# A fused matmul and batch norm on one core: an affine chain reordered, statistics taken in advance, and one output block moved behind the last matmul

## The chip, the cores and the metric

The kernel runs on one core of a Trainium2 chip. The metric is the device time of one execution in microseconds (us), told as the median of several. The profile shows one execution. Its span runs from the first to the last instruction and is about 1.8 us shorter than the time of the same execution (218.9 us against 220.69 before). A run is called slow when it lies over 1.5% above the fastest of its kernel.

Engines: PE is TensorE's matmuls, PEld its weight loads, DVE is VectorE, ACT is ScalarE, POOL is GpSimd, and SP issues the stores.

## The reference

```python
# x: 16 x 512 x 1024, weight: 1024 x 768, gamma, beta: 768, all float32
y = np.matmul(x, weight)
mean = np.mean(y, axis=(0, 1), keepdims=True)
var = np.var(y, axis=(0, 1), keepdims=True)
y_norm = (y - mean) / np.sqrt(var + eps)
return (gamma * y_norm + beta).astype(np.float32)     # 8192 rows x 768 columns, 25.2 MB
```

Each of the 768 columns needs its mean and variance over all 8192 rows before its first value can be stored.

## The kernel before

The columns are six tiles of 128 (nt = 0 to 5), the rows sixteen chunks of 512 (c). Tiles 0 to 2 are done first, with rows on the partitions. Their statistics end at about 126 us. From there on their output is made (VectorE multiplies by the scale, GpSimd adds the shift), while TensorE multiplies tiles 3, 4 and 5. Those three have their columns on the partitions, are normalized in place, transposed by TensorE, copied from PSUM to SBUF by ScalarE and stored. Every instruction is placed on its engine by an event with a time in a list that is sorted, so an event's time is an order and not a clock.

The affine numbers of a finished tile, and its normalization:

```python
def finish(nt):
    one = slice(nt, nt + 1)
    seq(nc.vector.bn_aggr(mv[:, nt, :], stats[:, nt, :, :]))
    seq(nc.scalar.activation(std[:, one], mv[:, nt, 1:2], AF.Sqrt, bias=eps_sb, scale=1.0))
    seq(nc.vector.scalar_tensor_tensor(
        tmp[:, one], mv[:, nt, 0:1], -1.0, gamma_sb[:, one], op0=ALU.mult, op1=ALU.mult,
    ))
    seq(nc.vector.reciprocal(rstd, std[:, one]))
    seq(nc.vector.tensor_mul(scale[:, one], rstd, gamma_sb[:, one]))
    seq(nc.vector.scalar_tensor_tensor(
        shift[:, one], tmp[:, one], rstd, beta_sb[:, one], op0=ALU.mult, op1=ALU.add,
    ))
# norm(nt, c, eng): y = y * scale + shift, in place, on VectorE ("dve") or ScalarE ("act")
# norm_rows: ring <- y * scale, VectorE.   shift_rows: ring <- ring + shift, GpSimd, in place.
```

The first affine chain, and the events of the three last tiles:

```python
S = pe
at(S + 0.9, affine_rows)                  # sums, scale, shift of tiles 0 to 2
at(S + 4.4, spread_rows, 0)               # scale as a row, by a matmul
for nt in range(GA):
    at(S + 2.4, norm, nt, 0, "dve")
at(S + 2.5, shift_diag)
at(S + 5.2, spread_rows, 1)               # shift as a row: GpSimd starts behind it
...
for b in range(C // 2):                   # outputs(nt, t0, step): tiles 3 and 4
    tb = t0 + step * b
    for i in range(2):
        at(tb - 2.2 + 0.5 * i, norm, nt, 2 * b + i, "act" if tb < tr + 2.0 and i == 0 else "dve")
    at(tb, turn_y, (nt,), 2 * b * CH, 2 * RT)
    at(tb + 2.2, out_copy, (nt,), 2 * b * CH, "act")
    at(tb + 2.3, store, (nt,), 2 * b * CH, 2 * RT)
```

```python
singles = ctx.enter_context(tc.tile_pool(name="singles", bufs=1))
xtpool = ctx.enter_context(tc.tile_pool(name="xtpool", bufs=C - EARLY))
...                                       # singles: 20 tiles in all; of these:
ones = singles.tile([P, P], f32)          # only column 0 is read
stats = singles.tile([P, NT, C, 6], f32)
msq = singles.tile([P, GA], f32)
...
if late:                                  # out_copy of tile 5
    o_sb = xtpool.tile([P, tiles, cols], f32, tag="xT")
else:                                     # all other outputs: pieces of the ring in singles
    o_sb = piece(tiles * cols).rearrange("p (s n) -> p s n", n=cols)
```

## Time and profile before

| | before |
|---|---|
| median of three runs (range) | 221.04 us (220.65 to 222.17) |
| span of the profiled run | 218.9 us |
| statistics of tiles 0 to 2 begin to be joined (S) | 126.48 us |
| last matmul ends (E) | 199.75 us |
| behind it, to the end of the span | 19.16 us |

S here and below is the measured start of the first aggregate of the first affine chain (the code's S is an event time), and the differences are taken from the trace's own times. The page's slices, 40 equal parts of 5.5 us, tenths busy for TensorE and GB/s of all transfers:

```profile
PE   7998999999999999999999979999999988995900
GB/s 60 175 204 190 194 196 196 197 196 196 194 191 197 195 196 196 198 189 10 0 4 0 0 0 14 340 308 257 269 258 360 295 353 334 346 346 347 201 345 244
```

The reader sees TensorE at 8 or 9 tenths nearly throughout, loads at about 196 GB/s in the first half, a pause of seven slices, and then stores that run at about 346 GB/s and break once (201), one slice behind the one where TensorE falls to 5.

### The profile page before, as it was taken

The numbers are of one execution on the slowest core, as the hardware profiler recorded it, in microseconds if no ns is written. First come the engines' busy times: TensorE is split into PE (matmuls) and PEld (weight loads), VectorE is DVE, ScalarE is ACT, GpSimd is POOL, SyncE is SP. The second block draws the span as 40 slices with busy tenths as digits, with TensorE's granted clock in tenths as the row PEclk, the third lists the DMA queues.
The fourth block names the chain that finished last, engine by engine and source line by source line (L and its number), as shares of the span: only waits on it lengthen the run. The fifth ranks groups of instructions, "written<-read, shape, count | busy, mean of one in ns | idle before, by whom it ended". The sixth has DMA issues, their size and how long they took to land.

```text
span 218.9 us, 3417 instructions
## 1 busy us (share of the span) xinstructions
PE 198.5 (91%) x1154; PEld 105.2 (48%) x1170; DVE 155.7 (71%) x264; ACT 119.8 (55%) x220; POOL 134.0 (61%) x153
## 2 busy tenths in 40 slices
PE   7998999999999999999999979999999988995900
PEld 3453545454544555546555534444444545651900
DVE  3223788897978789998554287889989999745800
ACT  2001454554543566636666225776676887985850
POOL 8897595977765799935559103999899953000000
PEclk9999999999999999999999999999999999999795
DMA  5999999999999999990000000986769899999698
GB/s 60 175 204 190 194 196 196 197 196 196 194 191 197 195 196 196 198 189 10 0 4 0 0 0 14 340 308 257 269 258 360 295 353 334 346 346 347 201 345 244
DMA packets 70161, 43.75 MB, mean 200 GB/s; under 512 B 4096, under 2 KB 69632, under 8 KB 70144
## 3 DMA queue, kind: packets, MB, share of 16 engines
q0 software_dynamic: 34624, 18.36, 61.1%
q1 hardware_dynamic: 35520, 25.18, 35.7%
q8 instruction: 9, 0.15, 0.3%
q14 instruction: 8, 0.07, 0.1%
HBM read 36.71 MB, written 25.17 MB: 283 GB/s over the span
## 4 chain that ended last, share of the span: by engine, by line
PE 64%; DVE 10%; POOL 8%; DMA 6%; issue 4%; ACT 3%; ACTq 0%; DVEq 0%; POOLq 0%
PE y_ps L190 31%; PE y_ps L180 29%; POOL ring L280 6%; PE o_ps L340 3%; ACT o_sb L353 3%; DVE stats L299 3%; DMA w_sb<-in_weight_dram 3%; DVE ring L274 2%; DVE y_sb L324 2%; DMA ring<-in_x_dram 2%; POOL w_sb L143 2%; DMA out_dram<-ring 1%; POOL ring L156 1%; DVE mv L306 1%; PE a_ps L266 1%
## 5 line engine op out<-in xcount | busy, mean ns | idle before, releaser
L190 PE MATMUL y_ps<-xT_sb,w_sb 128*128 128x512 bf16 (+1 forms) x477 | 117.5, 381 | 2.6 <-DMA w_sb<-in_weight_dram 1.4
L190 PEld LDWEIGHTS <-w_sb 128*128 128x128 bf16 x492 | 46.7, 96 | 60.8 <-issue 3.1
L302 ACT CAST y_sb<-y_ps 128x512 bf16<-128x512 f32 x60 | 35.4, 590 | 53.3 <-DVE stats L299 51.4
L180 PE MATMUL y_ps<-w_sb,xT_sb 128*128 128x384 bf16 x384 | 63.4, 326 | 0.0
L299 DVE BATCH_NORM_STATS2 stats<-y_ps 128x6 f32<-128x512 f32 x60 | 40.6, 684 | 22.5 <-PE y_ps L190 22.3
L280 POOL TENSOR_TENSOR ring<-ring,sum 128x768 f32<-128x768 f32 x24 | 43.5, 1847 | 17.9 <-ACT sum L268 14.0
L156 POOL DMA_DIRECT2D ring<-in_x_dram x72 | 45.2, 633 | 11.7 <-DVE xT_sb L168 6.1
L180 PEld LDWEIGHTS <-xT_sb 128*128 128x128 bf16 x384 | 37.5, 98 | 25.6
L206 POOL TENSOR_TENSOR sum<-sum,sq_sb 128x384 f32<-128x384 f32 x38 | 38.0, 1000 | 18.0 <-ACT sq_sb L202 16.8
L168 DVE STREAM_TRANSPOSE xT_sb<-ring 128x1024 f32<-128x1024 f32 (+1 forms) x34 | 39.5, 1167 | 12.0 <-DMA ring<-in_x_dram 12.0
L340 PE MATMUL o_ps<-ident,y_sb 128*128 128x128 bf16 x240 | 37.3, 230 | 5.5 <-DVE y_sb L324 5.2
L209 DVE TENSOR_TENSOR sum<-y_ps,sum 128x384 f32<-128x384 f32 x48 | 26.1, 544 | 14.6 <-ACT sq_sb L202 13.8
L202 ACT ACTIVATE sq_sb<-y_ps 128x384 f32<-128x384 f32 x48 | 23.4, 492 | 14.9 <-PE y_ps L180 11.4
L215 ACT CAST y_sb<-y_ps 128x384 bf16<-128x384 f32 x48 | 22.9, 476 | 7.5 <-DVE sum L209 7.3
L353 ACT CAST ring<-o_ps 128x1024 f32<-128x1024 bf16 (+1 forms) x24 | 22.5, 960 | 4.9 <-PE o_ps L340 2.5
L340 PEld LDWEIGHTS <-y_sb 128*128 128x128 bf16 x240 | 20.6, 104 | 9.1 <-DVE y_sb L324 7.3
L274 DVE TENSOR_TENSOR ring<-y_sb,a_ps 128x768 f32<-128x768 bf16 x24 | 22.3, 938 | 0.2 <-PE a_ps L266 0.2
L324 DVE TENSOR_SCALAR y_sb<-y_sb,scale,shift 128x512 bf16<-128x512 bf16 x43 | 17.3, 457 | 0.0
L319 ACT ACTIVATE y_sb<-y_sb,shift,scale 128x512 bf16<-128x512 bf16 x17 | 13.3, 813 | 0.1
L149 PE MATMUL idle_ps<-idle_sb 128*128 128x512 bf16 x37 | 9.8, 429 | 1.2 <-DVE idle_sb L100 1.2
L353 ACT CAST o_sb<-o_ps 128x512 f32<-128x512 bf16 x16 | 7.9, 679 | 1.2 <-PE o_ps L340 1.2
L149 PEld LDWEIGHTS <-idle_sb 128*128 128x128 bf16 x38 | 4.0, 108 | 6.4 <-issue 1.9
(45 smaller groups left out, 35.9 us busy)
## 6 DMA issues: line engine op xcount, KB each, us to landing
ring<-in_x_dram POOLq DMA_DIRECT2D x56, 256.0 KB, 8.5
out_dram<-ring SPq DMA_DIRECT2D x32, 384.0 KB, 2.9
out_dram<-ring SPq DMA_DIRECT2D x16, 512.0 KB, 5.9
out_dram<-o_sb SPq DMA_DIRECT2D x16, 256.0 KB, 3.3
ring<-in_x_dram POOLq DMA_DIRECT2D x16, 128.0 KB, 5.2
w_sb<-in_weight_dram POOLq DMA_DIRECT2D x8, 96.0 KB, 4.6
w_sb<-in_weight_dram POOLq DMA_DIRECT2D x4, 192.0 KB, 5.4
gamma_sb<-in_gamma_dram SPq DMA_DIRECT2D x6, 0.5 KB, 4.8
```

Of the source, the lines that this page charges most:

```text
L156: seq(nc.gpsimd.dma_start(x_bf[32 * i:32 * i + 32], src[:, :, KQ * i:KQ * (i + 1)]))
L168: seq(nc.vector.transpose(dst[:, half, :, jw0:jw1], src[:, :, jw0:jw1]))
L180: seq(nc.tensor.matmul(y_ps, xT[c][:, jw, s * P:(s + 1) * P, e], w_sb[:, jw, e, 0:NA], start=(jw == 0 and e == 0), stop=(jw == JW - 1 and ...
L190: seq(nc.tensor.matmul(y_ps, w_sb[:, jw, e, nt * P:(nt + 1) * P], xT[c][:, jw, q0 * QR:q1 * QR, e], start=(jw == 0 and e == 0 and q0 == 0) ...
L206: seq(eng.tensor_add(acc, acc, py.pop(("sq", c, s))))
L209: seq(nc.vector.tensor_add(sum1, py["row", c, s][:, 0:NA], sum1))
L274: seq(nc.vector.tensor_mul(o_sb, yrow[c][:, s:s + 2], aff[0][:, None, :].to_broadcast([P, 2, NA]),))
L280: seq(nc.gpsimd.tensor_add(o_sb, o_sb, sum1[:, None, :].to_broadcast([P, 2, NA])))
L299: seq(nc.vector.bn_stats(stats[:, nt, i, :], py[nt, c]))
L302: seq(nc.scalar.copy(y(nt, c), py.pop((nt, c))))
L340: seq(nc.tensor.transpose(dst, src, ident))
L353: seq(nc.scalar.copy(o_sb, src))
```

## The change

Its intent is to take waits off TensorE's path and to keep the stores going. Four parts: (1) in the first affine chain the three normalizations go behind the shift diagonals and the first rows' multiply, so that GpSimd starts earlier; (2) in the finishes of tiles 3 and 4, three one-element instructions go from VectorE to ScalarE; (3) the last 512 KB output block of tile 4 is held back and transposed behind the last matmul; (4) of tile 5, the statistics of fourteen chunks are joined ahead and the last chunk is multiplied and summed up by halves. Three small tiles are new. The core of the diff:

```diff
+    HELD = 1
...
     stats = singles.tile([P, NT, C, 6], f32)
+    ngamma = singles.tile([P, NT], f32)
+    nscale = singles.tile([P, 1], f32)
+    fin = singles.tile([P, 21], f32)
...
+    def sum_up():
+        seq(nc.vector.memset(fin[:, 0:1], float((C - 2) * CH)))
+        seq(nc.vector.bn_aggr(fin[:, 1:3], stats[:, NT - 1, 0:C - 2, :]))
+        seq(nc.vector.tensor_scalar(
+            fin[:, 2:3], fin[:, 2:3], float((C - 2) * CH), None, op0=ALU.mult))
...        (mm_half, bn_half, keep_half: the last chunk in two halves of 256)
+    def finish_var(nt):
+        one = slice(nt, nt + 1)
+        seq(nc.vector.bn_aggr(mv[:, nt, :], stats[:, nt, :, :]))
+        seq(nc.scalar.activation(std[:, one], mv[:, nt, 1:2], AF.Sqrt, bias=eps_sb, scale=1.0))
+        seq(nc.vector.reciprocal(rstd, std[:, one]))
+
+    def finish_affine(nt):
+        one = slice(nt, nt + 1)
+        seq(nc.scalar.activation(nscale, rstd, AF.Identity, scale=ngamma[:, one]))
+        seq(nc.scalar.activation(scale[:, one], rstd, AF.Identity, scale=gamma_sb[:, one]))
+        seq(nc.scalar.activation(
+            shift[:, one], mv[:, nt, 0:1], AF.Identity, bias=beta_sb[:, one], scale=nscale))
...
     at(S + 0.9, affine_rows)
+    at(S + 2.4, shift_diag)
     at(S + 4.4, spread_rows, 0)
+    at(S + 5.6, spread_rows, 1)
     for nt in range(GA):
-        at(S + 2.4, norm, nt, 0, "dve")
-    at(S + 2.5, shift_diag)
-    at(S + 5.2, spread_rows, 1)
+        at(S + 5.0, norm, nt, 0, "dve")
     ga = tuple(range(GA))
-    tr, tk = S + 5.3, S + 3.9
+    tr, tk = S + 4.7, S + 6.3
...
-            tk += 9.6 if c else 8.6
+            tk += 9.6 if c else 7.2
...
+            if nt == NT - 2 and b >= C // 2 - HELD:
+                held.append(b)
+                continue
...        (held_outputs: the held block's events, from t0 = E on)
-        at(pe + 0.55, finish, nt)
+        if nt < NT - 1:
+            at(pe + 0.55, finish_var, nt)
+            at(pe + 1.6, finish_affine, nt)
+        else:
+            at(pe + 0.55, finish, nt)
```

More of the change, by code (lines that the diff above doesn't have):

```diff
@@ L297, in bn, with mm_half, bn_half, keep_half @@
     def bn(nt, c):
+        if (nt, c) == (NT - 1, C - 2):
+            seq(nc.vector.bn_stats(fin[:, 3:9], py[nt, c]))
+            return
         i = c if nt >= GA else COLS.index(c)
         seq(nc.vector.bn_stats(stats[:, nt, i, :], py[nt, c]))
+    def sum_up():
[3 more added lines that the diff above has]
+            fin[:, 2:3], fin[:, 2:3], float((C - 2) * CH), None, op0=ALU.mult))
+    def mm_half(q):
+        y_ps = psum.tile([P, CH], f32, tag="b")
+        py["half", q] = y_ps[:, 0:QR]
+        for jw in range(JW):
+            for e in range(2):
+                seq(nc.tensor.matmul(
+                    y_ps[:, 0:QR], w_sb[:, jw, e, (NT - 1) * P:NT * P],
+                    xT[C - 1][:, jw, q * QR:(q + 1) * QR, e],
+                    start=(jw == 0 and e == 0), stop=(jw == JW - 1 and e == 1),
+                ))
+    def bn_half(q):
+        seq(nc.vector.bn_stats(fin[:, 9 + 6 * q:15 + 6 * q], py["half", q]))
+    def keep_half(q):
+        seq(nc.scalar.copy(y(NT - 1, C - 1)[:, q * QR:(q + 1) * QR], py.pop(("half", q))))
     def keep(nt, c):
         seq(nc.scalar.copy(y(nt, c), py.pop((nt, c))))
+    def negate_gamma():
+        seq(nc.vector.tensor_scalar(ngamma, gamma_sb, -1.0, None, op0=ALU.mult))
+    def finish_var(nt):
[9 more added lines that the diff above has]
+            shift[:, one], mv[:, nt, 0:1], AF.Identity, bias=beta_sb[:, one], scale=nscale))
     def finish(nt):
         one = slice(nt, nt + 1)
-        seq(nc.vector.bn_aggr(mv[:, nt, :], stats[:, nt, :, :]))
+        src = stats[:, nt, :, :] if nt < NT - 1 else fin
+        seq(nc.vector.bn_aggr(mv[:, nt, :], src))
         seq(nc.scalar.activation(std[:, one], mv[:, nt, 1:2], AF.Sqrt, bias=eps_sb, scale=1.0))
@@ L452 @@
     S = pe
+    at(S - 30.0, negate_gamma)
     at(S + 0.9, affine_rows)
+    at(S + 2.4, shift_diag)
     at(S + 4.4, spread_rows, 0)
+    at(S + 5.6, spread_rows, 1)
     for nt in range(GA):
-        at(S + 2.4, norm, nt, 0, "dve")
-    at(S + 2.5, shift_diag)
-    at(S + 5.2, spread_rows, 1)
+        at(S + 5.0, norm, nt, 0, "dve")
     ga = tuple(range(GA))
-    tr, tk = S + 5.3, S + 3.9
+    tr, tk = S + 4.7, S + 6.3
     for c in range(C):
@@ L485, in outputs, with held_outputs @@
             at(tb + 2.3, store, (nt,), 2 * b * CH, 2 * RT)
+    def held_outputs(nt, t0):
+        for i, b in enumerate(held):
+            for j in range(2):
+                at(t0 - 3.0 + 0.4 * (2 * i + j), norm, nt, 2 * b + j, "dve")
+            at(t0 + 0.05, turn_y, (nt,), 2 * b * CH, 2 * RT)
+            at(t0 + 0.7 + 0.1 * i, out_copy, (nt,), 2 * b * CH, "act")
+            at(t0 + 0.75 + 0.1 * i, store, (nt,), 2 * b * CH, 2 * RT)
     def last_outputs(nt, t0):
@@ L494, in last_outputs @@
             at(tb + 0.6, store, (nt,), c * CH, RT)
+    held = []
     halves = [range(JW // 2), range(JW // 2, JW)]
@@ L498 @@
         for c in range(EARLY, C):
+            if (nt, c) == (NT - 1, C - 1):
+                for q in range(QPC):
+                    at(pe, mm_half, q)
+                    pe += 0.9
+                    at(pe + 0.2, bn_half, q)
+                    at(pe + (0.4 if q == 0 else 1.0), keep_half, q)
+                at(pe - 2.4, sum_up)
+                continue
             for jws in halves:
                 unit(nt, c, MM_US / 2 + (0.12 if nt == GA else 0.17), jws)
-        at(pe + 0.55, finish, nt)
+        if nt < NT - 1:
[3 more added lines that the diff above has]
+            at(pe + 0.55, finish, nt)
         if nt == GA:
@@ L506 @@
         else:
+            held_outputs(nt - 1, pe)
             last_outputs(nt, pe + 3.0)
```

## The prediction

> **What bounds the kernel now.** I read the slices of the page first, then the chain of waits, then the waits of TensorE, then the stretches of the output phase, then the tail's timeline. The kernel has two halves. Up to about 126 us it loads x and multiplies; the change touches nothing there. From 126 us on it multiplies the last three column tiles (n = 3, 4, 5) and at the same time normalizes and stores everything. Waits of TensorE from 126 to 203 us (releaser, total, times, longest):
>
> ```profile
> PE o_ps L340 <- DVE y_sb L324: 5.2, 4, 2.7
> ```
>
> The timeline gives the four: 1.20 us before 130.86 (behind the affine chain of the first three tiles), 0.69 before 179.47, 0.59 before 182.70, and 2.71 in the tail. The first three sum to 2.48 us, and TensorE is otherwise busy from 126 to the last matmul at 199.76. Busy time per stretch (engines, granted clock, DMA share, GB/s):
>
> ```profile
> 136.00:173.00 37.00, 36.74 (x202) 17.33 (x205) 33.46 (x49) 25.77 (x41) 35.65 (x21) 1.00 0.78 289
> 173.00:202.70 29.70, 25.45 (x195) 14.23 (x198) 22.85 (x46) 23.77 (x34) 6.94 (x4) 0.99 1.11 347
> 202.70:206.60 3.90, 3.90 (x47) 3.90 (x45) 3.90 (x14) 3.49 (x8) 0.00 (x0) 0.61 0.49 144
> 206.60:217.20 10.60, 1.14 (x21) 0.97 (x18) 0.65 (x3) 4.44 (x10) 0.00 (x0) 0.78 1.15 346
> ```
>
> The reader is to see that the stores run at 346 GB/s from 173 us to the end, except for 3.9 us at 144 GB/s. Lost there: 3.9 x (346 - 144) / 346 = 2.3 us. Ahead of 173 the stores are short of supply, with POOL at 35.65 of 37 us. Why the queue runs dry at 202.7 is seen in the tail's timeline:
>
> ```profile
> 199.79 0.70 DVE L299 BATCH_NORM_STATS2 stats<-y_ps 128x6 f32<-128x512 f32 x1 [1.11 <-PE y_ps L190]
> 200.52 0.59 DVE L306 BATCH_NORM_AGGREGATE mv<-stats 128x2 f32<-128x96 f32 x1
> 201.14 0.29 ACT L307 ACTIVATE std<-mv,eps_sb 128x1 f32<-128x1 f32 x1 [1.84 <-DVE mv L306]
> ...
> 201.99 1.70 DVE L324 TENSOR_SCALAR y_sb<-y_sb,scale,shift 128x512 bf16<-128x512 bf16 x5
> 202.46 1.09 PEld L340 LDWEIGHTS <-y_sb 128*128 128x128 bf16 x11 [3.23 <-DVE y_sb L324]
> 202.46 1.25 PE L340 MATMUL o_ps<-ident,y_sb 128*128 128x128 bf16 x10 [2.71 <-DVE y_sb L324]
> 203.11 0.59 ACT L353 CAST o_sb<-o_ps 128x512 f32<-128x512 bf16 x1 [1.20 <-PE o_ps L340]
> ```
>
> The last matmul E ends at 199.76; its statistics, aggregate, square root, scale, shift and first normalization take until 202.42, and the first store is issued at 203.72 = E + 3.96. So two limits lie close together: TensorE up to E plus this chain, and store bandwidth from 173 us on.
>
> **What the Trainium skill says.** "SBUF — State Buffer", section "Who interferes with whom": a VectorE instruction with two SBUF inputs, or in a two-port mode, and a GpSimd instruction that reads SBUF exclude each other for a whole instruction. The trace agrees. One-element instructions of the two middle finishes last as long as the GpSimd adds beside them:
>
> ```profile
> 173.34 1.18 DVE L308 SCALAR_TENSOR_TENSOR tmp<-mv,gamma_sb 128x1 f32<-128x1 f32 x1
> 174.62 1.68 DVE L312 TENSOR_TENSOR scale<-rstd,gamma_sb 128x1 f32<-128x1 f32 x1
> 154.48 21.80 POOL L280 TENSOR_TENSOR ring<-ring,sum 128x768 f32<-128x768 f32 x12 [1.09 <-DVE ring L274]
> ```
>
> The second ends at 176.30, the block of adds at 176.28; alone (in the tail, with GpSimd finished) the same two take 0.16 us each. "ScalarE: Activation LUTs", section "What ACT_TABLE_LOAD costs": an ACTIVATE costs 186 ns and 93 ns per pointer operand, plus 0.833 ns per element; the square root with one pointer shows 0.29 us, so it agrees. "HBM Reference", section "Specifications (TRN2)": 358 GB/s per core as share, more when a core streams alone; the trace shows 345 to 347 in this stage, taken as the cap. "TensorE: Matmul & The Clock Gate", section "What's actually happening": the clock halves after an idle window. The trace shows the granted clock at 0.58 from 202 to 204 us, just behind the 2.71 us gap.
>
> **The change, part by part.** The instruction order of both kernels tells what moves.
>
> (1) First affine chain. The three normalizations of 1.04 us leave their place ahead of the shift diagonals and come after the first rows' multiply. The transposes start later on TensorE: before, 25 matmuls at 0.227 us after the sums and then a wait; now 28 matmuls (to 124.00 + 28 x 0.227 = 130.36), the scale broadcast, 4 more, the shift broadcast (about 131.7), 5 more (133.3), then the first transpose. The scale diagonals are done at 129.62, so the first broadcast does not wait; the shift diagonals are done about 131.1, so nor does the second; normalized data come about 132.9. The wait of 1.20 us goes. ScalarE's copy of the shift row, which starts GpSimd, moves from 134.51 to about 132.3, so GpSimd starts its 24 adds (1.85 us each) about 2.2 us earlier.
>
> (2) Finishes of tiles 3 and 4. Three one-element instructions leave VectorE for three small ACTIVATEs, by the page 0.28 to 0.37 us each, about 0.75 with overlap, ScalarE having gaps there. VectorE gets back 153.47 - 152.0 = 1.5 us in the first finish and 176.36 - 173.9 = 2.5 us in the second (173.9: aggregate, square root, reciprocal remain). Both waits of TensorE at 179.47 and 182.70 end with a normalization that VectorE reached late and that was itself blocked by GpSimd (1.90 us for two at 177.83; 2.81 for five at 181.12). VectorE then comes 2.5 us sooner and GpSimd's last add ends about 177 rather than 182.5. I take both waits, 1.28 us, as gone, and allow some remainder below.
>
> (3) One 512 KB block of tile 4 held back. Eight interleaved transposes leave the stretch before E. A pair takes 0.281 us against 0.227 for a matmul alone: 8 x 0.055 = 0.44 us earlier E. Behind E they run in TensorE's gap, about 0.5 us, then one ScalarE copy of 1.01 us. Its store goes out about E + 2.05.
>
> (4) Last statistics. 13 chunks plus one are aggregated before E into one triple; the last chunk is done by halves. Behind E remain a half (estimate 0.69 - 256 / 0.96 ns = 0.42 us instead of 0.69) and an aggregate over 21 values (0.205 us, from the row with 24, instead of 0.59). Together 0.66 us less. The 16 half matmuls of 256 columns cost TensorE what 8 whole ones do.
>
> Sum on TensorE: E = 199.76 - 1.20 - 1.28 - 0.44 = 196.8. Behind E: the held store starts the queue at E + 2.05 plus 0.9 us (before: issue at 203.72, data from about 204.6), followed by 1.5 us of data, then the 4.19 MB of the last tile, 12.1 us, then 1.65 us to the end (217.25 to 218.9). That gives E + 18.2 = 215.0 in the span.
>
> The other limit, store bandwidth: without the hole of 2.3 us the span would be 218.9 - 2.3 = 216.6, less whatever earlier supply brings. TensorE brings tile 3's blocks 1.2 us earlier, GpSimd its rows 2 to 3 us; I take 1.3 us, giving 215.3. The two limits meet at about 215.3. Unfinished parts (a remaining wait at 179, ScalarE short for copies, a small hole at the end) I put at 0.3: span 215.6. The median lies 2.1 us above the profiled span before (221.04 against 218.9): **217.6 us**, 1.5% faster.
>
> **Rivals.** (a) Store bandwidth alone decides and supply does not come earlier: only the hole closes, span 216.6, 218.7 us. For it: the queue is full from 173 on and ring buffers must be stored before they are overwritten. Against it: ahead of 173 the stores run at 289 GB/s only, so they were short of supply. (b) A new wait takes the place of the one removed: the later normalizations of the first tiles now lie inside GpSimd's adds and are blocked for up to 1.8 us each, TensorE waits before its first transpose, and 1.2 us come back: about 218.8 us. For it: the normalizations at 177.83 were so blocked. Against: GpSimd can start only when they have nearly ended. (c) ScalarE becomes the bound: it is busy 5.00 of 5 us from 185 to 195 and gets six small instructions more; then PSUM banks come free late. Against it: those six lie at about 150 and 172, where it has gaps, and one block copy (1.01 us) leaves the crowded stretch; cost at most 0.5 us. (d) Everything arrives and earlier supply is worth the full 2 us: span 214.6, 216.7 us, right at the 2% line of 216.6.
>
> **Range and chances.** From (d) with a little more, 216.3, to (a) and (b) together, 219.3. Faster by over 2% needs all parts and a supply gain over 2 us: 0.15. Slower needs a new serial wait of over 7 us, which nothing suggests: 0.01. Within 2%: 0.84.
>
> **What would show each step.** (1) TensorE without a wait near 130, GpSimd's adds starting near 133. (2) No VectorE instruction of one element over 0.5 us; no TensorE wait near 178 and 182. (3) A group of 72 transposes behind the last matmul, E near 196.8. (4) First normalization ending near E + 2.0 (before 2.66); the hole of 3.9 us at 144 GB/s nearly gone. If E falls as told but the end does not follow, bandwidth is the bound (rival a). If TensorE waits for normalized data near 133 us, rival b. The prediction is wrong if the removed waits return elsewhere on TensorE or if VectorE stays late through the locks of GpSimd.

## The result, and the profile after

| | before | after |
|---|---|---|
| median of six runs (range) | 221.13 us (220.65 to 222.17) | 219.84 us (219.51 to 225.25) |
| span of the profiled run | 218.9 | 218.2 |
| S | 126.48 | 127.94 |
| E - S | 73.27 | 69.66 |
| end - E | 19.16 | 20.58 |
| end - S | 92.43 | 90.24 |

The ratio is 0.9934, with a 95% interval of 0.9909 to 0.996. A ratio here is the mean time of one kernel's fast runs over that of the other's in the same rounds, so it is not quite the ratio of the medians. One of the six runs after, 225.25 us, is slow and not in the ratio; it was not profiled. The predicted gain was 3.4 us and the measured one 1.3 us. 219.84 lies 0.5 us above the range of 216.3 to 219.3.

The slices of the page after:

```profile
PE   7997999999999999999999999999999999996500
GB/s 64 161 180 178 192 196 195 197 196 196 196 190 194 197 196 196 196 196 67 0 5 0 0 0 0 241 376 312 286 300 366 256 343 342 347 347 323 306 288 199
```

TensorE has no slice below 9 from the fifth to the thirty-sixth, so the dips are gone. But where the stores ran at 345 before, they now run at 306 and 288. The waits of TensorE from 120 us to the end are down to one line (releaser, total, times, longest):

```profile
PE o_ps L388 <- DVE y_sb L372: 1.7, 1, 1.7
```

The stretches of the output phase, with the same bounds and columns as in the prediction:

```profile
136.00:173.00 37.00, 36.74 (x208) 17.58 (x210) 32.93 (x47) 27.13 (x46) 37.00 (x22) 1.00 0.81 300
173.00:202.70 29.70, 27.78 (x238) 16.96 (x241) 22.70 (x56) 26.02 (x42) 5.21 (x3) 1.00 1.10 341
202.70:206.60 3.90, 2.26 (x28) 1.50 (x28) 1.81 (x6) 3.90 (x9) 0.00 (x0) 1.00 1.05 300
206.60:217.20 10.60, 0.00 (x0) 0.00 (x0) 0.00 (x0) 1.55 (x4) 0.00 (x0) 0.59 0.96 270
```

The third stretch has lost its hole (300 instead of 144 GB/s). The fourth moves less than before (270 instead of 346; it ends with idle time here, so a better measure follows below). The tail's timeline and GpSimd's block of adds:

```profile
197.64 0.43 DVE L327 BATCH_NORM_STATS2 fin<-y_ps 128x6 f32<-128x256 f32 x1 [0.48 <-PE y_ps L320]
198.11 0.25 DVE L354 BATCH_NORM_AGGREGATE mv<-fin 128x2 f32<-128x21 f32 x1
...
199.25 5.26 DVE L372 TENSOR_SCALAR y_sb<-y_sb,scale,shift 128x512 bf16<-128x512 bf16 x16
199.72 5.25 PE L388 MATMUL o_ps<-ident,y_sb 128*128 128x128 bf16 x64 [1.66 <-DVE y_sb L372]
```

```profile
134.61 43.59 POOL L284 TENSOR_TENSOR ring<-ring,sum 128x768 f32<-128x768 f32 x24 [12.06 <-ACT sum L272]
```

The last half's statistics take 0.43 us and the aggregate 0.25, as estimated (0.42 and 0.205). GpSimd does its 24 adds without one wait and ends at 178.20, 4.3 us ahead of the 182.5 of before. So TensorE's side came as predicted. What was lost lies in the stores behind E and, in this pair of traces, ahead of S, which came 1.46 us later.

### The profile page after: what moved, and what is told of

Read it like the earlier page. It is cut to its first block, busy times and chain, and to the rows that moved or that the text cites. A ratio compares the mean times of both kernels' runs of the same rounds, so it can differ in the third digit from the quotient of the medians.

```text
span 218.2 us, 3442 instructions
## 1 busy us (share of the span) xinstructions
PE 199.1 (91%) x1162; PEld 105.2 (48%) x1178; DVE 151.5 (69%) x264; ACT 120.4 (55%) x226; POOL 134.4 (62%) x153
## 4 chain that ended last, share of the span: by engine, by line
PE 74%; DVE 6%; DMA 5%; ACT 4%; POOL 3%; issue 3%; DVEq 0%; POOLq 0%
PE y_ps L194 40%; PE y_ps L184 29%; ACT o_sb L401 3%; PE o_ps L388 3%; DMA w_sb<-in_weight_dram 3%; DVE y_sb L372 3%; DMA ring<-in_x_dram 3%; POOL w_sb L147 2%; DVE ring L278 1%; DVE stats L306 1%; POOL ring L160 1%; PE y_ps L320 1%; PE a_ps L270 1%; PE tot_ps L230 1%; ACT ring L401 0%
## 5 line engine op out<-in xcount | busy, mean ns | idle before, releaser
L194 PE MATMUL y_ps<-xT_sb,w_sb 128*128 128x512 bf16 (+1 forms) x469 | 115.3, 382 | 2.8 <-DMA w_sb<-in_weight_dram 1.5
L194 PEld LDWEIGHTS <-w_sb 128*128 128x128 bf16 x484 | 46.1, 96 | 60.6 <-issue 3.4
L333 ACT CAST y_sb<-y_ps 128x512 bf16<-128x512 f32 x59 | 34.7, 589 | 52.3 <-DVE stats L306 49.5
L306 DVE BATCH_NORM_STATS2 stats<-y_ps 128x6 f32<-128x512 f32 x58 | 39.2, 685 | 21.7 <-PE y_ps L194 21.4
L284 POOL TENSOR_TENSOR ring<-ring,sum 128x768 f32<-128x768 f32 x24 | 43.6, 1854 | 12.1 <-ACT sum L272 12.1
L210 POOL TENSOR_TENSOR sum<-sum,sq_sb 128x384 f32<-128x384 f32 x38 | 38.2, 1006 | 18.2 <-ACT sq_sb L206 16.9
L388 PE MATMUL o_ps<-ident,y_sb 128*128 128x128 bf16 x240 | 36.2, 219 | 1.9 <-DVE y_sb L372 1.7
L388 PEld LDWEIGHTS <-y_sb 128*128 128x128 bf16 x240 | 19.0, 97 | 4.9 <-DVE y_sb L372 1.8
L367 ACT ACTIVATE y_sb<-y_sb,shift,scale 128x512 bf16<-128x512 bf16 x16 | 12.6, 812 | 0.0
L153 PE MATMUL idle_ps<-idle_sb 128*128 128x512 bf16 x37 | 11.2, 472 | 1.2 <-DVE idle_sb L101 1.2
```

The source lines that it names most:

```text
L194: seq(nc.tensor.matmul(y_ps, w_sb[:, jw, e, nt * P:(nt + 1) * P], xT[c][:, jw, q0 * QR:q1 * QR, e], start=(jw == 0 and e == 0 and q0 == 0) ...
L210: seq(eng.tensor_add(acc, acc, py.pop(("sq", c, s))))
L284: seq(nc.gpsimd.tensor_add(o_sb, o_sb, sum1[:, None, :].to_broadcast([P, 2, NA])))
L306: seq(nc.vector.bn_stats(stats[:, nt, i, :], py[nt, c]))
L333: seq(nc.scalar.copy(y(nt, c), py.pop((nt, c))))
L388: seq(nc.tensor.transpose(dst, src, ident))
```

## The experiments

Twelve kernels ran, in three sets, each on another chip (0, 6 and 1). Each is compared with runs of the kernel before on its own chip in the same rounds. All gave correct results. For the slow stores behind E there were three theories at the start: the queue is slower when it never runs empty, one issuing queue is the limit, or it is a matter of the chip or of chance. A fourth, the place of the tiles in SBUF, came out of the first set. The expectations quoted here use short names of their own for the theories.

### Both kernels again: a_again and b_again

No edit.

> The changed kernel, unaltered, for a second trace. In its first trace the last matmul came 70.3 us after the first-tile statistics began to close (the statistics instruction ahead of the first affine chain), 3.6 us less than before, but the stores of the last tile landed one every 0.915 us (286 GB/s) where before they landed one every 0.76 us (345 GB/s), and the first half took 1.5 us longer (127.33 against 125.86). Theory 1 (a consequence of the change: the store queue no longer runs empty ahead of the last tile, and is then fed more slowly): the 0.9 us per store shows again, time about 219.8. Theory 2 (chance of one run): the pace is back at 0.76 us and the span near 216. On the first half: if it is chance, it comes out between 125.9 and 127.5 and the kernel before shows the same spread; if it is the change, 127.3 again.

> The kernel before, unaltered, for a second trace. If the first half differs by chance alone, its first-tile statistics close anywhere from 125.9 to 127.5; if the changed kernel is really slower there, it is at 125.9 again. The stores of the last tile should land one every 0.76 us again, after a hole of some 2 us in which the DMA engines run empty.

Measured on chip 0: after 224.9 us (224.07 to 225.61, six runs), before 221.94 (221.24 to 222.75, eleven runs), ratio 1.0127, interval 1.0102 to 1.0153. **On this chip the changed kernel is slower.** The before kernel looks as it did: span 219.5, E - S 73.26, end - E 19.19. The changed one has E - S 75.32 instead of 69.66, and end - E 20.59, as on the first chip. So there are two separate things: one ahead of E that struck here and not there, and one behind E that is in both.

*Ahead of E.* Look at what VectorE does with the first normalization of tile 3. The changed kernel is one and the same program on both chips. Before, first chip:

```profile
166.89 0.40 DVE L324 TENSOR_SCALAR y_sb<-y_sb,scale,shift 128x512 bf16<-128x512 bf16 x1
```

After, first chip, the first two of these normalizations:

```profile
166.29 1.02 DVE L372 TENSOR_SCALAR y_sb<-y_sb,scale,shift 128x512 bf16<-128x512 bf16 x1
...
168.70 0.45 DVE L372 TENSOR_SCALAR y_sb<-y_sb,scale,shift 128x512 bf16<-128x512 bf16 x1
```

After, chip 0, the same two and the multiply between them:

```profile
164.69 2.81 DVE L372 TENSOR_SCALAR y_sb<-y_sb,scale,shift 128x512 bf16<-128x512 bf16 x1
167.41 0.94 DVE L278 TENSOR_TENSOR ring<-y_sb,a_ps 128x768 f32<-128x768 bf16 x1
...
168.89 1.53 DVE L372 TENSOR_SCALAR y_sb<-y_sb,scale,shift 128x512 bf16<-128x512 bf16 x1
```

And GpSimd's adds of chip 0, which were one block of 24 on the first chip:

```profile
133.00 34.34 POOL L284 TENSOR_TENSOR ring<-ring,sum 128x768 f32<-128x768 f32 x19 [12.07 <-ACT sum L272]
168.43 1.83 POOL L284 TENSOR_TENSOR ring<-ring,sum 128x768 f32<-128x768 f32 x1 [1.09 <-DVE ring L278]
```

In both traces of the changed kernel this normalization starts 38.35 us behind S, in the same part of a GpSimd add: (166.29 - 134.61) / 1.816 us = 17.44 adds on the first chip, so 0.44 of an add has passed and 0.56, or 1.02 us, is left. There it takes just these 1.02 us: it ends as the running add ends. On chip 0 it takes 2.81, one add of 1.8 us more, so GpSimd's next add went first. The multiply that GpSimd needs comes behind the normalization on VectorE, so GpSimd then runs out of work and waits 1.09 us; its add begins just ahead of the next normalization and blocks it for 1.53 us. The two engines now go in step, one round of 2.93 us (from one multiply's start, 167.41, to the next one's, 170.34) instead of the 1.85 of one add. Five waits of GpSimd result, and TensorE pays for them when the data of tile 3 come late. Waits from 165 to 186 us:

```profile
POOL ring L284 <- DVE ring L278: 5.0, 5, 1.1
...
PE o_ps L388 <- ACT y_sb L367: 2.2, 1, 2.2
```

Two more TensorE waits of 0.5 us lie ahead of it, at 173.4 and 176.3, and the granted clock is 0.5 from 181.1 to 184.5 behind it. I call such a run *struck*. The struck trace's E - S is 5.66 us longer. (Not all of it is the lock's own: e_align2 below is struck too, keeps the full clock there, and has E - S 73.87.)

*Behind E.* In the changed kernel the 16 last stores land 0.92 us apart on both chips, once they are even, against 0.76 before: 256 KB per 0.915 us is 286 GB/s and per 0.757 us 346 GB/s.

### The held block back in its place: e_held0

```diff
-    HELD = 1
+    HELD = 0
```

> The changed kernel with no block held back (all eight blocks of the fifth tile ahead of the last matmul). The last matmul then ends 0.44 us later. Theory 1 (slow feeding comes from a queue that does not run empty): the queue runs empty again for 1.5 to 2.5 us, the last tile's stores land one every 0.76 us, and the kernel is as fast as the changed one or up to 1.5 us faster, 218.3 to 219.8. Rival (the slow pace has nothing to do with the hole): pace stays 0.9 us, and the time rises by 0.5 to 1.5 us, to 220.3 or more.

Measured on chip 0: 225.16 us (223.8 to 228.36, two of six slow), ratio 1.0099 (1.0068 to 1.013), struck as well (E - S 75.76). The hole is back, with a gap of 2.11 us on TensorE, so the queue did run empty, and yet the stores behind it land 0.92 us apart. The first theory falls: the pace has nothing to do with a hole.

### Half of the last stores on another queue: e_actq

```diff
+        eng = nc.scalar if nts == (NT - 1,) and (m0 // CH) % 2 else nc.sync
-        seq(nc.sync.dma_start(
+        seq(eng.dma_start(
```

> The changed kernel with every second store of the last tile issued from ScalarE's queue instead of the sync engine's. Theory 1a (one queue hands out stores at 0.915 us each): two queues hand out twice as fast, the last tile's stores run at 345 GB/s again, and the span falls by up to 2.4 us, to about 217.5. Rival (the DMA engines or memory themselves are slower there, whatever the queue): 0.9 us per store on average remains, time 219.8, or worse because ScalarE issues beside its copies.

Measured on chip 0: 224.75 us (224.12 to 226.3), ratio 1.0126 (1.0095 to 1.0156), struck (E - S 75.30), end - E 20.68, still 0.92 us per store on average. The second theory falls. As chip 0 runs the before kernel at 0.76, chip and chance fall too for this part.

### The place in SBUF, both ways: e_align and b_shift

What remains is what the stores read. The program as built tells where the tiles lie: before, the lowest of the late output tiles begins at byte 61952 of each partition, which is 121 x 512 (the others lie 8192 bytes apart); after, at 62112, because the three new small tiles take 32 + 32 + 96 bytes per partition. Each store reads rows of 128 float32, 512 bytes. The Trainium skill's "DMA: Bandwidth & Descriptors", section "How a descriptor splits into AXI transactions", says that a transaction "must start from a 256B-aligned address" and that bytes fetched below the start are thrown away and still cost: 512 bytes from 160 bytes behind a boundary would then need three transactions instead of two. I had not looked at addresses when I predicted. e_align is the changed kernel with 160 bytes less in a tile of which one column is used; b_shift is the kernel before with 160 bytes more:

```diff
# e_align: after, and
-    ones = singles.tile([P, P], f32)
+    ones = singles.tile([P, P - 40], f32)
# b_shift: before, and
     warm = singles.tile([P, 1], f32)
+    pad = singles.tile([P, 40], f32)
+    seq(nc.vector.memset(pad[:, 0:1], 0.0))
```

> The changed kernel with its three new small tensors paid for out of another tensor (a constant of which one column is used loses 160 bytes per partition), so that the output tiles of the last column tile start at byte 61952 of the partition again, a multiple of 512, as in the kernel before. In the changed kernel they start at 62112, 160 bytes further. Nothing else moves: the instruction order is the same. Theory A (start address): DMA reads of 512 bytes that start 160 bytes off a 256-byte border are slower; with the border restored the last stores land every 0.76 us instead of 0.92, and the end comes 2.3 us sooner after the last matmul (about 18.3 us instead of 20.6). Rival (anything else in the tail): 0.92 stays. Theory B (locks of VectorE by GpSimd near 165 us, which cost the second set of runs some 5 us) is untouched by this: where it strikes, it strikes here too, and the time is 222.5 on such a chip, 217.5 otherwise.

> The kernel before with 160 unused bytes per partition added ahead of the output tiles of the last column tile, which moves them from byte 61952 to 62112 as in the changed kernel. Theory A: its last stores land every 0.92 us instead of 0.76, 15 intervals of 0.16 us, so it is 2.0 to 2.4 us slower than before: 1.0 percent. Rival: no change, within 0.3 us.

Measured on chip 6 (before: 221.66 us, 220.32 to 222.29): e_align 223.37 (222.25 to 224.76), ratio 1.0087 (1.002 to 1.0153), struck (E - S 76.56); b_shift 224.8 (223.04 to 226.5, one of four slow), ratio 1.0174 (1.0104 to 1.0243). The stretch of the last stores, in this order: before and after on the first chip, e_align and b_shift (last column GB/s):

```profile
207.00:217.00 10.00, 0.74 (x14) 0.57 (x11) 0.25 (x1) 4.04 (x9) 0.00 (x0) 0.78 1.15 346
```

```profile
205.00:215.00 10.00, 0.00 (x0) 0.00 (x0) 0.00 (x0) 3.15 (x7) 0.00 (x0) 0.68 1.03 288
```

```profile
210.00:220.00 10.00, 1.85 (x25) 1.68 (x23) 0.87 (x3) 4.44 (x10) 0.00 (x0) 0.67 1.15 346
```

```profile
207.00:219.00 12.00, 0.97 (x17) 0.75 (x14) 0.51 (x2) 4.30 (x9) 0.00 (x0) 0.73 1.02 286
```

**Shown both ways**: moving these tiles, and what is laid out behind them, by 160 bytes takes 346 to 286 GB/s in the old kernel, and back to 346 in the new one. In b_shift end - E is 21.26 us instead of 19.16, 2.1 us more. In e_align it is 18.22, just what the prediction had (E + 18.2), against 20.59 in a_again: 2.4 us. Both e_align and a_again are struck, on different chips; end - E also hangs on how early E comes, and e_align2, the program of e_align, has 19.98. All other stores read the ring, which lies ahead of the new tiles, and kept their pace. That it is the third transaction which costs is not shown: in the trace after, one DMA engine that lags behind the others lands its parts of the first eight displaced stores 0.76 us apart, and takes 0.92 only once it has caught up.

### Which part of the change leads to the striking: e_noaff and e_fin

Both are e_align with one part undone. e_noaff has the first affine chain's events as before; e_fin has the finish on VectorE for all tiles:

```diff
# e_noaff: e_align, and the event lines of the diff from S + 2.4 to tk back to (7.2 to 8.6 as well)
     at(S + 4.4, spread_rows, 0)
     for nt in range(GA):
         at(S + 2.4, norm, nt, 0, "dve")
     at(S + 2.5, shift_diag)
     at(S + 5.2, spread_rows, 1)
     tr, tk = S + 5.3, S + 3.9
# e_fin: e_align, and
-        if nt < NT - 1:
-            at(pe + 0.55, finish_var, nt)
-            at(pe + 1.6, finish_affine, nt)
-        else:
-            at(pe + 0.55, finish, nt)
+        at(pe + 0.55, finish, nt)
```

> The aligned changed kernel with the first affine chain, its normalizations and the transposes of the first three tiles put back where the kernel before has them; the finishes of tiles 3 and 4, the last statistics and the held block stay changed. Theory B1 (the reordered first chain lets GpSimd start 2 us earlier and so puts VectorE's first normalization of tile 3 in the middle of a GpSimd add, where it can lose a second turn): the locks near 165 us go, all normalizations there take under 0.6 us, while the TensorE wait of 1.2 us near 131 comes back; 1.2 us slower than the aligned kernel where that one is not struck, 3 us or more faster where it is. Rival B2 (the locks come from the finish moved to ScalarE, or strike at random): normalizations of 1.5 us and more appear here too.

> The aligned changed kernel with the finishes of tiles 3 and 4 put back on VectorE as in the kernel before; all else stays changed. If the finish moved to ScalarE shifts VectorE into the middle of a GpSimd add (theory B2), the first normalization of tile 3 meets GpSimd late in an add, takes 0.4 to 0.5 us, and no run shows the lock; the one-element instructions are blocked for 1 to 2.9 us per finish instead, and TensorE waits some 1.3 us again: end about 90.5 us after the first aggregate, 219 us. If the lock is there whatever the finish, 223 again.

Measured, e_noaff on chip 6: 219.11, 225.23, 220.76 and 226.16 us; the second and fourth count as slow, the ratio of the two others is 0.9929 (0.9845 to 1.0012). The profiled one was not struck: E - S 71.21, with the wait of 1.2 us near 130 back. But its first normalization of tile 3 takes as long as that of the changed kernel:

```profile
166.42 1.03 DVE L372 TENSOR_SCALAR y_sb<-y_sb,scale,shift 128x512 bf16<-128x512 bf16 x1
```

The two slow runs have no profile; their times fit struck ones, but that is not shown. So the early arrival stays without the new order of the first chain. Measured, e_fin on chip 1 (before: 221.5 us, 220.61 to 222.55): 219.32 us (219.15 to 219.62), ratio 0.9915 (0.9888 to 0.9942). Its first and fourth normalizations of tile 3:

```profile
165.25 0.75 DVE L372 TENSOR_SCALAR y_sb<-y_sb,scale,shift 128x512 bf16<-128x512 bf16 x1
...
171.28 2.06 DVE L372 TENSOR_SCALAR y_sb<-y_sb,scale,shift 128x512 bf16<-128x512 bf16 x1
```

The second and third take 0.46 and 0.45 us, so one long wait stays single and the lock step does not set in. The four runs lie within 0.5 us of each other, while e_align2, with the finish on ScalarE, took about 4 us more in all four of its runs in the same rounds. So it is the finish moved to ScalarE that goes with the striking. What it changes is the part of the add in which this normalization arrives. With the finish on VectorE, GpSimd waits once for VectorE in the finish of tile 3 (1.36 us ahead of 153.21 in e_fin, 1.09 ahead of 154.48 before) and its adds lie later from then on: the normalization arrives when 0.63 of an add has passed in e_fin ((165.25 - 153.21) / 1.816 = 6.63) and 0.83 before ((166.89 - 154.48) / 1.816 = 6.83), where it takes 0.40 us. With the finish on ScalarE that wait is gone, and it arrives at 0.44 after and at 0.43 in e_noaff. That the early arrival is what exposes VectorE to the second add is argued from these four, not shown by itself. The price of e_fin: TensorE's waits of 1.16 us at 178.8 and 0.54 at 180.7 are back, and E - S is 71.64.

### Normalizations off VectorE: e_actnorm, e_act3, and e_align again

If the lock is the cause, normalizations on ScalarE must remove it (beside the adds they take 0.81 to 0.82 us each in e_act3). e_actnorm moves seven of tiles 3 and 4, e_act3 only the four of tile 3 that lie beside the adds. e_align2 is e_align once more, for chip 1:

```diff
# e_actnorm: e_align, and
-  norm, nt, 2 * b + i, "act" if tb < tr + 2.0 and i == 0 else "dve")
+  norm, nt, 2 * b + i, "act" if tb < tr + 2.0 else "dve")
# e_act3: e_align, and
+  norm, nt, 2 * b + i, "act" if tb < tr + 2.0 and (i == 0 or nt == GA and b < 4) else "dve")
```

> The aligned changed kernel with both normalizations of a block on ScalarE for as long as GpSimd's adds run (7 of them leave VectorE), so that VectorE has no two-port instruction beside GpSimd. Theory B: no VectorE normalization over 0.6 us and no GpSimd wait before 178 us; the last matmul comes 70 us after the first aggregate on every chip, the time 217 to 218. Rival: ScalarE is too full (4.2 of 5 us busy there) and TensorE waits for it: 0.5 to 2 us slower than the unstruck kernel, 218 to 219.5, and TensorE shows waits on ScalarE near 170 to 180.

> The aligned changed kernel once more, as the control of this set and for another draw of the lock. Theory B: VectorE's first normalization of tile 3 starts some 38 us after the first aggregate in the middle of a GpSimd add; when the add ends either side may get the ports. If VectorE does (the first trace of the changed kernel), the last matmul comes about 69.7 us after the first aggregate, the end about 89 us after it, and the time is near 217.5; if GpSimd does (the second set and the first aligned run), 76 us, 94.8 us and 223.

> The aligned changed kernel with only the four VectorE normalizations of tile 3 that lie beside back-to-back GpSimd adds (those near 166 to 176 us) moved to ScalarE. Theory B (those four hold the loss): GpSimd runs its 24 adds without a wait, TensorE has no wait of 2.2 us near 180, runs agree within 1.5 us, last matmul 69.7 to 71 us after the first aggregate, time 217 to 218.5. Rival: ScalarE is filled by them (0.82 us each against 0.45 on VectorE) and TensorE waits for its copies, 219 to 220.5, as with seven moved.

Measured: e_actnorm on chip 6, 220.79 us (219.69 to 221.11), ratio 0.9958 (0.9904 to 1.0012): not struck, but TensorE waits for ScalarE, 0.89 us at 179.3 and 0.54 at 182.8 (E - S 71.69). That is a small form of rival (c). On chip 1, e_align2 took 223.11 us (222.72 to 223.92), ratio 1.0089 (1.0056 to 1.0123), and its first normalization of tile 3 is blocked (E - S 73.87, end - E 19.98):

```profile
165.51 2.94 DVE L372 TENSOR_SCALAR y_sb<-y_sb,scale,shift 128x512 bf16<-128x512 bf16 x1
```

Beside it in the same rounds, **e_act3 took 218.59 us (218.42 to 219.36), ratio 0.9887 (0.9856 to 0.9918)**, the fastest of all, with all four runs within 1 us. Its adds on GpSimd, and its stretch behind the last matmul:

```profile
134.64 41.56 POOL L284 TENSOR_TENSOR ring<-ring,sum 128x768 f32<-128x768 f32 x23 [12.05 <-ACT sum L272]
```

```profile
202.70:206.60 3.90, 2.23 (x28) 1.47 (x27) 1.77 (x6) 3.89 (x8) 0.00 (x0) 1.00 1.15 345
```

23 adds go without a wait, TensorE waits only once, in the tail, and E - S is 69.59, as in the unstruck run after (69.66). e_align2 and e_act3 differ by those four normalizations alone, and by 4.5 us. The stores run at 345 GB/s in the place of the hole.

### The tail alone: e_tail

e_align with both the first chain (as in e_noaff) and the finish (as in e_fin) undone; what stays is the held block and the advance statistics.

> The kernel before with the last statistics in advance and by halves and the held block alone, aligned; first chain and the finishes of tiles 3 and 4 as before. The last matmul is 0.44 us earlier than before (72.8 us after the first aggregate), the chain behind it 0.66 us shorter, the hole of 3.9 us gone. If store bandwidth alone decides, the hole of 2.3 us is the gain, 219.2 us; if the trailing DMA engine that the hole let catch up costs it back, only 0.5 to 1 us, 220.5.

Measured on chip 1: 220.32 us (219.94 to 221.18), ratio 0.9962 (0.9921 to 1.0003). TensorE's three old waits are there (1.20, 0.73, 0.59) and E is 199.90. The hole is closed:

```profile
202.70:206.60 3.90, 3.90 (x51) 2.73 (x51) 3.90 (x13) 3.90 (x9) 0.00 (x0) 1.00 1.11 334
```

Against 144 GB/s before, that is 3.9 x (334 - 144) / 346 = 2.1 us more moved. Yet end - S falls only from 92.43 (before, first chip) to 91.79, by 0.64 us, and the median by 1.2 us (221.5 to 220.32, with an interval that just reaches no change). Where the rest went shows in the landings of each store in the trace. A store lands in 16 parts, one for each DMA engine. While the queue is full, one part, which I take to be that of one engine, lands 1.93 us behind the first in the kernel before, at the same pace, and during the hole it catches up: spread 0.17 us behind it. So the first engines stood idle for about 2 us in the hole, but the trailing one for only 0.74 us (0.21 in b_again), and the end is the landing of the last. In e_tail that engine stands idle for 0.00 us, and the last tile's spread is 0.83 us; in e_act3 1.50. (b_again has the same end - S as before, 92.45: its trailing engine landed the last store ahead of the hole 0.57 us later behind S, and so had less to wait.)

## Why the prediction was wrong, point by point

| trace (unless said, fast) | E - S | end - E | end - S | us per last store |
|---|---|---|---|---|
| before, first chip | 73.27 | 19.16 | 92.43 | 0.76 |
| predicted | 70.3 | 18.2 | 88.5 | 0.76 |
| after, first chip | 69.66 | 20.58 | 90.24 | 0.92 |
| after, chip 0 (struck) | 75.32 | 20.59 | 95.91 | 0.92 |
| e_align, chip 6 (struck, aligned) | 76.56 | 18.22 | 94.78 | 0.76 |
| e_align2, chip 1 (struck, aligned) | 73.87 | 19.98 | 93.84 | 0.76 |
| e_act3, chip 1 (neither) | 69.59 | 20.01 | 89.60 | 0.76 |

(The predicted row takes E 196.8 and end 215.0 less the S of before, 126.48; with the 0.3 us put on and the bandwidth limit, the prediction's end - S was 215.6 - 126.48 = 89.1. Its last sum has a slip: 215.6 + 2.1 is 217.7.)

**Part (1), the first chain: right.** The 1.20 us wait is gone in every trace with the new order and back in e_noaff. GpSimd starts 6.7 us behind S against 8.6. Rival (b), that these normalizations be blocked, did not come at this place.

**Part (2), the finishes: right where the run is not struck.** The waits at 179.47 and 182.70 are gone in the profiled run after and in e_act3, and both have successors in e_fin. But the step "GpSimd's last add ends about 177 rather than 182.5" holds only there (178.2); in a_again it ends at 181.6. I had named "VectorE stays late through the locks of GpSimd" as what would make the prediction wrong and put no number on it; it came in the four normalizations of tile 3 and is worth 4.3 us of E - S in e_align2 and 5.66 in a_again, where the clock fell as well. On chip 0 it made the kernel 1.3% slower than before, an outcome that the range did not hold. On the first chip it explains none of the fast runs; the one slow run fits it but has no profile.

**Part (3) and the chain behind E in (4): right.** The 72 transposes are there, E - S is even 0.6 us shorter than predicted, and the first normalization starts 1.64 us behind E (199.25 - 197.61). (The code joins 14 chunks ahead of E, where the prediction says "13 chunks plus one".)

**"Then the 4.19 MB of the last tile, 12.1 us": this term failed.** It assumed 346 GB/s for stores whose addresses the change moves by 160 bytes. The leading engines land them 0.915 us apart, 16 x 0.915 = 14.6 us. The trailing engine, on which the end hangs, lands its sixteen parts in 13.34 us in the trace after (75.74 to 89.08 us behind S), against 12.11 in e_act3 with aligned tiles: **the term was 1.2 us too small**. end - E does not measure it alone: the aligned kernel has 18.22 in e_align, 19.98 in e_align2 and 20.01 in e_act3, because an early E leaves more stores behind it.

**"Without the hole of 2.3 us the span would be 216.6": this term was mis-sized, and so was the 1.3 us for earlier supply.** The hole's loss was computed from the mean rate of 16 engines, while the end hangs on the one that trails. That engine stood idle for 0.74 us in the hole, 0.21 in the second trace, and e_tail measures 0.64 us of end - S for closing it: about 1.6 us too much. Supply was too small by as much: the trailing engine landed the last store ahead of tile 5 at 78.42 us behind S before and at 75.74 after, 2.68 us sooner instead of 1.3. From S on the traces gained 2.68 + 0.74 - 1.23 = 2.19 us; the prediction had 1.3 + 2.3 - 0.3 = 3.3. With right addresses the changed kernel would have come to 3.4 by this sum (an estimate), so the prediction would have been met from S on, but **by luck**, because two errors cancel. e_act3, with right addresses and no lock, gained 2.09 + 0.74 = 2.83.

Of the miss of 2.24 us (219.84 against 217.6) the traces so put 1.14 behind S (90.24 against 89.1), which the addresses explain. The rest is 1.46 us by which S came later in the profiled run after than before, less about 0.35 by which the median lies nearer to the profiled span than the prediction put it. The prediction held that the change touches nothing ahead of S. S was 126.47 to 127.01 in the three traces whose first half is that of before (with b_shift), and 126.02 to 127.99 in the eleven others, on average half a microsecond later; whether the change has a part in that, or chance alone, stays open.

Open: what decides which of the two engines goes first when both wait at the end of an add (the same place in the add gave 1.02 us on one chip and 2.81 on another); which DMA engine trails, and why; and whether the slow run of 225.25 us was struck.

## What to carry to other kernels

A new small tile can shift every later buffer: before predicting a transfer's time, read the address of what it reads, and keep the place that it had (here a multiple of 512 bytes; 160 bytes behind it was slower, no other offset was tried). When a change moves work off an engine that another one can block, ask in which part of the other's instruction its next one will arrive; moving four such instructions to ScalarE was worth 4.5 us here where the lock had struck. And the loss by a hole in a transfer queue was here the idle time of the transfer engine that ends last, not the missing bytes over the mean rate. When a sum comes out right, check its terms one by one: here two were wrong by about 1.5 us each, in opposite directions.

## What the Trainium skill lacked or had wrong

- "DMA: Bandwidth & Descriptors", "How a descriptor splits into AXI transactions", is in line with the runs but gives no time: 512-byte reads that start 160 bytes behind a 256-byte boundary took 0.915 us per 256 KB store, aligned ones 0.757 us. No page says that small tiles in an earlier pool shift the start.
- "SBUF — State Buffer", "Who interferes with whom", says that "Whoever issues first gets the shared pair for the whole instruction". That does not tell who goes first at an add's end: VectorE arrived in the middle of an add, ahead of GpSimd's next one, and went first in one trace (1.02 us) and second in another (2.81 us). Nor does it say that the two can fall into step behind it (2.93 us a round instead of 1.85).
- "DMA: Bandwidth & Descriptors", "Latency and other measured facts", says that engines 7 and 15 are "Usually slower" and holds this to be specific to software-generated descriptors. Here one part of 16 trailed by 0.7 to 1.97 us at full pace in stores from the sync engine's queue, which the profile lists as hardware_dynamic; the trace does not tell which engine it is. It caught up when the queue ran dry (1.93 to 0.17 us before) or when the others slowed (1.32 to 0.34 after). No page gives such a lag or what it costs at the end.
